# Masked values of head 6 on VectorE in a two-layer recurrent trunk

## The chip, the cores and the metric

The kernel runs on one core of a Trainium2 chip. The metric is the device time of one execution in microseconds, the median of several. The core has TensorE (PE, with its weight loads as PEld), VectorE (DVE), ScalarE (ACT), GpSimd (POOL) and SyncE (SP, which here only issues DMAs). Each engine takes its instructions in a fixed order of its own; semaphores join them.

## The reference

Two layers of a decoder trunk in float32, width 1024: a gated linear recurrence with convolution (layer 0), then HGRN2, a gated linear attention with a matrix state for each of 8 heads (layer 1), then a norm. There are 1024 prompt tokens from an empty state, and 8 sample sequences of 4 tokens each with a state of their own, so 1056 tokens in all. The part that the change touches is the state of the sample sequences in layer 1:

```python
def _hgrn_layer(x, g_norm, w_in, lb, o_gain, w_out, S0):
    ...
    q, f, iv, gate = jnp.split(u, 4, axis=-1)
    ...
    k = -jnp.expm1(log_g)
    v = iv.reshape(Bsz, T, H_B, DV_B)
    o, S_T = _hgrn2_chunked(q, k, v, log_g, S0)
    o = o * lax.rsqrt(jnp.mean(o * o, axis=-1, keepdims=True) + EPS) * o_gain.reshape(H_B, DV_B).astype(jnp.float32)
    y = (o.reshape(Bsz, T, INNER_B) * jax.nn.silu(gate)).astype(x.dtype)
    return x + y @ w_out, S_T.astype(x.dtype)
```

Within `_hgrn2_chunked` a state moves on by

```python
S_new = jnp.exp(last[:, :, 0, :])[..., None] * S + jnp.einsum(
    'bhsk,bhsv->bhkv', kc * jnp.exp(last - cum), vc)
```

For a sample sequence the sum over `s` runs over its four tokens alone.

## The kernel before

**Products.** Every large product is made of three: operands are split into a rounded part and a rest (`xh`, `xl`; `whi`, `wlo`), ACT makes the rounded part by a cast (L433, L1574, L1739) and DVE or POOL the rest by a subtraction (L374). In layer 1 the input projection of a head is done by `seven`, with seven products in place of eight (a Strassen-like scheme over halves of the tokens and of the weights). A cell of its order, such as `3a`, is product 3 for the first half of the columns: 12 matmuls of 264 columns (L289 to L291) into one bank. Three banks go round for these cells. DVE adds a cell's result to what stands in the SBUF (L1651) and so frees its bank. The order for the last section of a head is `GV`, where each `*` is a burst of small products for the head before:

```python
GV = "1a 1b 6a 2a 2b 6b * 7a 7b 5a 5b 4a * 3a 3b 4b"
```

**Head after head.** In the section of head `h` the four bursts carry work for head `h` (the decay of its attention, level by level, in `scale` L1176 and the masks of L1198 and L1201) and for head `h - 1`: `burst1` brings its sample keys and values into place (`samples`, L1314), `burst2` its prompt states (`states`, with the scan L1375 and L1377) and the first half of the new sample states (`advance(h - 1, 0)`), `burst3` its outputs and the second half (`advance(h - 1, 1)`), `burst4` the gated result. The bursts of head 7 are in its last `seven` section; what follows after that section is the output projection, whose operands are read back from DRAM (`yd`) into `xl`, `k` and other tiles and split there, with bursts between its products.

**Masked values.** The 32 sample tokens lie in 96 rows (three parts each). To get the states of four sequences with one product, `masked(i)` multiplies the values `vst` with a 0/1 mask `bm` for each sequence, two sequences an instruction: `vb <- vst * bm`, 96 x 256 numbers, two instructions for `i = 0` (from `values`, in `burst1`) and two for `i = 1` (from `advance(h, 0)`, in `burst2`, into the same `vb` after PE has read it). PE then multiplies `kst` by `vb` (L1386), and DVE adds that to the decayed state `si` (L1393). They are made by POOL for heads 0 to 6 and by DVE for head 7, the last.

**What sets the order.** `Flow` is a planner that runs when the program is built. Each operation is added with its engine, an estimate of its duration, what it reads and writes, and a priority. `run` plans the whole list forward, then back and forward again eight times, and then tries 3000 random moves with a fixed seed and keeps what its own model calls no later. The best order is written out, and the engines follow it as it stands. PE's main products keep the order in which they were added. So a change of one operation's engine or length can move many rows of the other engines, and it does not move PE's. The estimate for an operation on DVE with two SBUF inputs can be marked to count POOL's use of the same port (`both`); the masked values aren't marked.

Of the kernel before, what the change touches and what calls it, by code (L numbers as in the profile page):

```python
# [55 lines left out]
H = 8  # L56
# [201 lines left out]
def tile_trunk(ctx: ExitStack, tc: tile.TileContext, xT, xN, prm, hc, w0, wg, wo0, w1, wo1, s_in,  # L258
# [86 lines left out]
    with ExitStack() as l0:  # L345
# [12 lines left out]
        def dma(dst, src, r=(), w=(), prio=5, kb=180, q=Q, chain=None):  # L358
            fl.add("SP" if q is Q else "ACT", 0.45, lambda: q.dma_start(dst, src), r, w, prio, kb * (1.0 if r or fl.exact else 0.75),
                   line=chain)  # L360
# [4 lines left out]
        def dve(n, emit, r, w, prio=5, both=False, chain=None):  # L365
            own = 0.135 if "scalar_tensor_tensor" in emit.__code__.co_names else 0.085
            fl.add("DVE", own + 0.00107 * n if fl.exact else 0.13 + 0.0011 * n, emit, r, w, prio, both=both, line=chain)
# [695 lines left out]
    with ExitStack() as l1:  # L1063
# [40 lines left out]
        def pe(us, emit, r, w):  # L1104
            fl.add("PE", us, emit, r, w, 1, main=True)

        def two(*name):
            return [(*name, i) for i in range(2)]
# [205 lines left out]
        def samples(o, ok, s, sk, a, dss, key, low, whole=None):  # L1314

            ps = s[:, a:a + 128]

            pe(0.17, lambda: T.matmul(ps[:96], o, ident, start=True, stop=True), ((ok,),), (sk,))
            yield
            act(128, lambda: S.copy(dss, ps[:96]), (sk,), ((key,),), 2)  # L1320
            w = slice(32 * low, 32 * low + 32)
            dve(128, lambda: V.tensor_tensor(dss[w], ps[w], dss[w].bitcast(F32), op=ALU.subtract), (sk, (key,)), ((key,),), 2)
            if whole is not None:
                act(128, lambda: S.copy(whole, ps[:32]), (sk,), (("vts",),), 2)

        def values(h, s, sk):
            yield from samples(vrep, "vrep", s, sk, 192, vst, "vst", 2, vts)
            masked(0, h == H - 1)

        def masked(i, last=False):  # L1330

            n = [96, 2, 128]
            for j in range(2):
                o, q = vb[:, 2 * j:2 * j + 2], slice(4 * i + 2 * j, 4 * i + 2 * j + 2)
                e = V if last else G
                (dve if last else pool)(256, lambda o=o, q=q, e=e: e.tensor_tensor(o, vst.bitcast(F32)[:, None, :].to_broadcast(n), bm[:, q, None].to_broadcast(n),
                                                           op=ALU.mult), (("vst",),), (("vb",),), 3)
# [45 lines left out]
        def advance(h, i):  # L1383

            ps, pk = next(hg)
            pe(0.36, lambda: T.matmul(ps, kst, vb.rearrange("p b v -> p (b v)"), start=True, stop=True),  # L1386
               (("kst",), ("vb",)), (pk,))
            yield
            if i == 0:
                masked(1, h == H - 1)  # L1390
            for n in range(4):
                b = 4 * i + n
                dve(128, lambda n=n, b=b: V.scalar_tensor_tensor(  # L1393
                    si[:, b, :], si[:, b, :], gp[:, h % 2, 8 + b:9 + b], ps[:, n * 128:(n + 1) * 128], op0=ALU.mult, op1=ALU.add),
                    (pk, ("gp", h % 2, 1)), (("si", i),), 4)
            if i:
                dma(ss_out[h], si.rearrange("p b v -> p (b v)"), two("si"), (), 6, 512)
# [68 lines left out]
        def burst1(h):  # L1466
            s = next(hg)
            run(together([*([levels01(h, *s)] if h < H else []), *([keys_(h - 1, *s), values(h - 1, *s)] if h else [])]))

        def burst2(h):  # L1470
            s = next(hg)
            run(together([*([levels24(h, *s)] if h < H else []), *([states(h - 1, *s), advance(h - 1, 0)] if h else [])]))

        def burst3(h):
            s = next(hg)
            run(together([*([outs(h - 1, *s), advance(h - 1, 1)] if h else []), *([levels816(h, *s)] if h < H else [])]))
# [487 lines left out]
```

## Time and profile before

| | us |
|---|---|
| median of 3 runs | 1040.65 (1040.01 to 1040.68) |
| the profiled execution | 1039.88 |
| its span (first to last instruction) | 1038.1 |
| TensorE busy | 1028.7 |
| VectorE busy | 790.2 |
| ScalarE busy | 591.0 |
| GpSimd busy | 500.1 |
| idle time of TensorE that ended with a wait for another engine | 2.9, in 3 waits |

The trace is of the one profiled execution; its span leaves out 1.8 us of start and end that the device time has. Starts are in us from the span's start. A row of a timeline has start, duration, engine, line, operation, the tile written, an arrow and the tiles read, then shapes; "x2" stands for two instructions in a row, and in square brackets stands the idle time before it and what ended it. A row of the waits says which engine's instruction waited for which: the sum in us, how many times, and the longest. A row of the windows has, for each stretch, the busy time of PE, PEld, DVE, ACT and POOL, then the granted TensorE clock, the share of the DMA engines and GB/s.

### The profile page before, as it was taken

The numbers are of one execution on the slowest core, as the hardware profiler recorded it, in microseconds if no ns is written. First come the engines' busy times: TensorE is split into PE (matmuls) and PEld (weight loads), VectorE is DVE, ScalarE is ACT, GpSimd is POOL, SyncE is SP. The second block draws the span as 40 slices with busy tenths as digits, with TensorE's granted clock in tenths as the row PEclk, the third lists the DMA queues.
The fourth block names the chain that finished last, engine by engine and source line by source line (L and its number), as shares of the span: only waits on it lengthen the run. The fifth ranks groups of instructions, "written<-read, shape, count | busy, mean of one in ns | idle before, by whom it ended". The sixth has DMA issues, their size and how long they took to land.

```text
span 1038.1 us, 25405 instructions
## 1 busy us (share of the span) xinstructions
PE 1028.7 (99%) x9794; PEld 999.5 (96%) x9794; DVE 790.2 (76%) x1543; ACT 591.0 (57%) x1349; POOL 500.1 (48%) x579
## 2 busy tenths in 40 slices
PE   9999999999999999999999999999999999999997
PEld 9999999999999999999999999999999999999986
DVE  6898996887897699255498986878879696985436
ACT  6678657867675775234355474637464545752334
POOL 2344453354433365643627555555645455641544
PEclk9999999999999999999999999999999999999998
DMA  8611112124742595444554241413233332756204
GB/s 280 195 47 39 53 52 76 58 61 121 232 158 61 175 284 169 146 162 153 190 167 143 95 146 44 161 59 135 78 111 105 103 127 83 232 183 207 87 1 168
DMA packets 92809, 133.55 MB, mean 129 GB/s; under 512 B 11728, under 2 KB 70096, under 8 KB 92688
## 3 DMA queue, kind: packets, MB, share of 16 engines
q1 hardware_dynamic: 82896, 115.50, 35.4%
q10 hardware_dynamic: 9792, 16.43, 4.8%
q8 instruction: 77, 1.26, 0.5%
q14 instruction: 44, 0.36, 0.1%
HBM read 88.81 MB, written 38.20 MB: 122 GB/s over the span
## 4 chain that ended last, share of the span: by engine, by line
PE 98%; issue 1%; POOL 0%; DVE 0%; POOLq 0%; ACT 0%; DVEq 0%
PE mm L289 27%; PE mm L291 27%; PE mm L290 27%; PE hg L1194 2%; PE hg L291 1%; PE hg L651 1%; PE hg L289 1%; PE hg L290 1%; PE hg L1409 1%; PE hg L1411 1%; PE hg L1357 1%; PE mm L1357 1%; PE hg L813 1%; PE hg L1453 1%; PE hg L1279 0%
## 5 line engine op out<-in xcount | busy, mean ns | idle before, releaser
L289 PE MATMUL mm<-xh,whi 128*128 128x352 f32 (+1 forms) x1127 | 351.9, 312 | 0.0
L291 PE MATMUL mm<-xh,wlo 128*128 128x352 f32 (+1 forms) x1127 | 347.9, 309 | 0.0
L290 PE MATMUL mm<-xl,whi 128*128 128x352 f32 (+1 forms) x1127 | 347.3, 308 | 0.0
L374 POOL TENSOR_TENSOR wlo<-wraw,whi 128x256 fp32r<-128x256 f32 (+3 forms) x180 | 196.7, 1111 | 192.7 <-ACT whi L433 104.0
L290 PEld LDWEIGHTS mm<-xl,whi 128*128 128x128 f32 x1127 | 212.3, 188 | 1.7
L289 PEld LDWEIGHTS mm<-xh,whi 128*128 128x128 f32 x1127 | 212.0, 188 | 1.9
L291 PEld LDWEIGHTS mm<-xh,wlo 128*128 128x128 f32 x1127 | 211.8, 188 | 0.1
L289 PE MATMUL mm<-t,whi 128*128 128x264 f32 (+1 forms) x330 | 96.9, 294 | 1.3 <-DVE sg L1651 1.3
L583 DVE SCALAR_TENSOR_TENSOR k<-xb,prm_sb,k 128x352 f32<-128x352 f32 (+2 forms) x144 | 87.6, 616 | 13.0 <-ACT k L580 7.9
L290 PE MATMUL mm<-t,whi 128*128 128x264 f32 (+1 forms) x330 | 94.4, 286 | 0.0
L291 PE MATMUL mm<-t,wlo 128*128 128x264 f32 (+1 forms) x330 | 94.4, 286 | 0.0
L374 POOL TENSOR_TENSOR wlo<-R,whi 128x256 fp32r<-128x256 f32 x78 | 66.8, 882 | 43.9 <-ACT whi L1574 32.2
L666 POOL TENSOR_TENSOR k<-X 128x352 f32<-128x352 f32 x36 | 43.4, 1216 | 59.3 <-DVE R L667 42.0
L1651 DVE TENSOR_TENSOR k<-mm,k 128x264 f32<-128x264 f32 x118 | 49.7, 425 | 22.9 <-PE mm L291 22.4
L289 PEld LDWEIGHTS mm<-t,whi 128*128 128x128 f32 x330 | 62.1, 188 | 2.6 <-DVE sg L1651 1.8
L291 PEld LDWEIGHTS mm<-t,wlo 128*128 128x128 f32 x330 | 62.2, 188 | 0.0
L290 PEld LDWEIGHTS mm<-t,whi 128*128 128x128 f32 x330 | 62.2, 188 | 0.0
L433 ACT CAST whi<-wraw 128x512 fp32r<-128x512 f32 (+2 forms) x79 | 44.0, 571 | 25.0 <-PE mm L290 9.3
L289 PE MATMUL mm<-yh,whi 128*128 128x352 f32 x153 | 50.0, 327 | 0.0
L291 PE MATMUL mm<-yh,wlo 128*128 128x352 f32 x153 | 49.4, 323 | 0.0
L290 PE MATMUL mm<-yl,whi 128*128 128x352 f32 x153 | 49.4, 323 | 0.0
L647 ACT ACTIVATE R<-hg,smalls 128x352 f32<-128x352 f32 x72 | 37.5, 552 | 16.2 <-DVE R L687 9.3
(481 smaller groups left out, 2497.9 us busy)
## 6 DMA issues: line engine op xcount, KB each, us to landing
wraw<-in_w_dram SPq DMA_DIRECT2D x54, 256.0 KB, 3.2
wraw<-in_w_dram ACTq DMA_DIRECT2D x34, 256.0 KB, 3.5
wraw<-in_wo_dram SPq DMA_DIRECT2D x34, 192.0 KB, 2.5
R<-in_w_dram ACTq DMA_DIRECT2D x19, 256.0 KB, 2.7
si<-in_s_in_dram SPq DMA_DIRECT2D x8, 512.0 KB, 5.6
vt<-sg SPq DMA_DIRECT2D x8, 512.0 KB, 3.7
sg<-vt SPq DMA_DIRECT2D x32, 128.0 KB, 2.9
kt<-kt SPq DMA_DIRECT2D x8, 512.0 KB, 2.7
```

The lines of the kernel that those rows point to most:

```text
L289: T.matmul(out, wh, xh, start=first, stop=False, skip_group_check=more)
L290: T.matmul(out, wh, xl, start=False, stop=False, skip_group_check=more)
L291: T.matmul(out, wl, xh, start=False, stop=last, skip_group_check=more)
L374: emit = lambda: e.tensor_tensor(b, x, a.bitcast(F32), op=ALU.subtract)
L433: act(m, lambda: S.copy(hi[:, :m], raw[:, :m]), rk, (hk,), prio, chain=chains[0])
L583: dve(u, lambda src=src, dst=dst, sh=sh, k=k: V.scalar_tensor_tensor(dst, sh(src, k), pc("cw", 12 * k + m), dst, op0=ALU.mult, op1=ALU.add ...
L647: act(CH, lambda ps=ps, R=R, i=i, j=j, hb=hb, m=m: S.activation(R[:, i, j], ps[:, :CH], AF.Tanh, bias=hb[:, m:m + 1], scale=0.5), (pk, ("s ...
L651: fl.add("PE", 0.62, lambda ps=ps, i=i, c=c: T.matmul(ps[:96, :CH], gs[:, i, :], ST[:96, chunk(c)], start=True, stop=True), (("gs",), *((" ...
L666: pool(CH, lambda x=x, a=a, b=b: G.tensor_tensor(x, a.bitcast(F32), b.bitcast(F32), op=ALU.add), (ak, bk), (xk,), 3)
L1194: T.matmul(ps[32 * j:32 * j + 32, n * w:n * w + w], B[:, o:o + 32], q(slice(o, o + 32)), start=True, stop=True, tile_position=(0, 32 * j))
L1357: T.matmul(ps[:, n * 128:(n + 1) * 128], kt[:, 4 * i + n, :], vt[:, 4 * i + n], start=True, stop=True)
L1651: dve(QT, lambda: V.tensor_tensor(o[0], z[0], u[0], op=ALU.add), (z[1], u[1]), (o[1],), 0)
```

## The change

Head 6 is added to the heads whose masked values DVE makes, in both places where `masked` is called:

```diff
         def values(h, s, sk):
             yield from samples(vrep, "vrep", s, sk, 192, vst, "vst", 2, vts)
-            masked(0, h == H - 1)
+            masked(0, h >= H - 2)
...
             if i == 0:
-                masked(1, h == H - 1)
+                masked(1, h >= H - 2)
```

The function that is called stays as it is:

```python
def masked(i, last=False):

    n = [96, 2, 128]
    for j in range(2):
        o, q = vb[:, 2 * j:2 * j + 2], slice(4 * i + 2 * j, 4 * i + 2 * j + 2)
        e = V if last else G
        (dve if last else pool)(256, lambda o=o, q=q, e=e: e.tensor_tensor(o, vst.bitcast(F32)[:, None, :].to_broadcast(n), bm[:, q, None].to_broadcast(n),
                                                   op=ALU.mult), (("vst",),), (("vb",),), 3)
```

The planner orders the rest anew. PE's 6325 rows stay the same. First, DVE in the last section of head 7, around burst 2: `xl<-xl,xh` are subtractions for operands of the output projection, `attnd` and `attns` the masks of the attention, `a` the prompt's state scan, `sg<-mm,k` the additions for the cells 3a and 3b, and `k<-mm,k` an addition for an earlier cell. Before:

```order
L374 TENSOR_TENSOR xl<-xl,xh 128x352
L1198 COPY_PREDICATED attnd<-mask_91,hg 128x256
L374 TENSOR_TENSOR xl<-xl,xh 128x352
L1201 COPY_PREDICATED attns<-mask_90,hg 32x32
L1375 COPY a<-hg 128x128
L1377 SCALAR_TENSOR_TENSOR a<-a,gp,hg 128x128 x2
L374 TENSOR_TENSOR xl<-xl,xh 128x352
L1377 SCALAR_TENSOR_TENSOR a<-a,gp,hg 128x128
L1651 TENSOR_TENSOR sg<-mm,k 128x264
```

The same stretch of DVE now, from the first masked values of head 6 to the mask behind the addition for 3a:

```order
L1336 TENSOR_TENSOR vb<-vst,bm 96x256 x2
L1651 TENSOR_TENSOR k<-mm,k 128x264
L374 TENSOR_TENSOR t_5166<-t_5166 128x352
L1651 TENSOR_TENSOR k<-mm,k 128x264
L374 TENSOR_TENSOR t_5166<-R,t_5166 128x352
L374 TENSOR_TENSOR xl<-R,xh 128x352
L374 TENSOR_TENSOR xl<-xl,xh 128x352 x2
L1651 TENSOR_TENSOR k<-mm,k 128x264
L1198 COPY_PREDICATED attnd<-mask_90,hg 128x256
L374 TENSOR_TENSOR xl<-xl,xh 128x352
L1651 TENSOR_TENSOR sg<-mm,k 128x264
L1198 COPY_PREDICATED attnd<-mask_91,hg 128x256
```

The masked values (`vb`) are new there; the third `xl` and the addition for 3a come ahead of a mask, of `attns`, and of the whole state scan.

Second, POOL at the same place; `wlo` are the rests of weights, `ab` a small copy behind a product of burst 2. Before:

```order
L1336 TENSOR_TENSOR vb<-vst,bm 96x256 x2
L374 TENSOR_TENSOR t_5169<-wraw,t_5169 128x128
L374 TENSOR_TENSOR t_5168<-t_5168 128x352
L374 TENSOR_TENSOR wlo<-wraw,whi 128x128
L1235 COPY ab<-R 128x8x4
L374 TENSOR_TENSOR xl<-xl,xh 128x352
L1336 TENSOR_TENSOR vb<-vst,bm 96x256 x2
L374 TENSOR_TENSOR wlo<-wraw,whi 128x512 x2
```

POOL now:

```order
L374 TENSOR_TENSOR t_5169<-wraw,t_5169 128x128
L374 TENSOR_TENSOR t_5168<-t_5168 128x352
L374 TENSOR_TENSOR wlo<-wraw,whi 128x128
L1235 COPY ab<-R 128x8x4
L374 TENSOR_TENSOR xl<-xl,xh 128x352
L374 TENSOR_TENSOR wlo<-wraw,whi 128x512 x2
```

Both pairs are gone; the other rows keep their order.

Third, DVE some rows later, at the scaling of the decays for head 7 (L1176) and the first additions of the output projection (L1779); a piece of the difference:

```order
 L1176 TENSOR_TENSOR R<-R,sg 128x64x8
+L1336 TENSOR_TENSOR vb<-vst,bm 96x256 x2
+L374 TENSOR_TENSOR xl<-k,xh 128x352
 L1176 TENSOR_TENSOR a<-sg 128x64x8
+L374 TENSOR_TENSOR t_5166<-k,t_5166 128x352
+L1779 TENSOR_TENSOR ST<-mm,ST 128x352
+L1779 TENSOR_TENSOR R<-mm,R 128x352
```

The second pair of masked values now stands here, ahead of the last scaling, with one subtraction. ACT has some casts and copies in another order nearby; SP issues the same DMAs, some of them in another order.

## The prediction

> **What bounds the kernel now.** I read the busy times of the engines first, then the chain of work that ended last, then what TensorE (PE) waited for, then windows and the timelines of the stretch that they point to.
>
> ```profile
> PE 1028.7 (99%) x9794; PEld 999.5 (96%) x9794; DVE 790.2 (76%) x1543; ACT 591.0 (57%) x1349; POOL 500.1 (48%) x579
> PE 98%; issue 1%; POOL 0%; DVE 0%; POOLq 0%; ACT 0%; DVEq 0%
> PE mm L289 <- DVE sg L1651: 1.3, 1, 1.3
> PE hg L813 <- DVE nr L501: 1.0, 1, 1.0
> PE hg L1833 <- DVE sg L1823: 0.6, 1, 0.6
> ```
>
> PE is busy in 1028.7 of 1038.1 us and is 98% of the chain. Nothing done on VectorE (DVE) or GpSimd (POOL) can change the time except through an idle gap of PE. The waits of PE are three, 2.9 us in all: one each at L813 and L1833 (the norms of layer 0 and the end of the program, far from the change), and one at L289, where a product waited for DVE's L1651. This last lies in the section of head 6, whose masked values the change moves. The windows around it (busy PE, weight load, DVE, ACT, POOL) show that it is the only gap of PE there:
>
> ```profile
> 895.00:908.00 13.00, 13.00 (x295) 12.31 (x293) 12.23 (x24) 8.35 (x22) 10.90 (x12) 1.00 0.84 257
> 908.00:913.00 5.00, 3.73 (x31) 3.47 (x28) 4.52 (x9) 2.28 (x5) 4.44 (x6) 1.00 0.59 192
> 913.00:985.00 72.00, 72.00 (x648) 69.72 (x647) 43.45 (x103) 26.08 (x87) 25.39 (x28) 1.00 0.51 159
> ```
>
> Timeline of PE there: start, duration, line. The cell 3a ends with the matmul at 909.66, 3b with that at 911.13, and 4b begins at 912.68.
>
> ```profile
> 909.66 0.28 PE L291 MATMUL mm<-xh,wlo 128*128 128x264 f32 x1
> 909.78 0.28 PE L289 MATMUL mm<-xh,whi 128*128 128x264 f32 x1
> ...
> 911.13 0.28 PE L291 MATMUL mm<-xh,wlo 128*128 128x264 f32 x1
> 912.68 0.39 PE L289 MATMUL mm<-t,whi 128*128 128x264 f32 x1 [1.27 <-DVE sg L1651]
> 912.91 0.28 PE L290 MATMUL mm<-t,whi 128*128 128x264 f32 x1
> ```
>
> Matmuls normally start 0.12 us apart (909.66 to 909.78). From 911.13 to 912.91 two steps took 1.78 us instead of 0.24, so the stop cost **1.54 us**; the idle gap alone is 1.27. 4b writes into the bank from which DVE's L1651 adds up 3a's result. 3a had been finished since 909.66 + 0.28 = 909.94, so the delay is DVE's. Its queue, and POOL's beside it:
>
> ```profile
> 906.38 0.58 DVE L374 TENSOR_TENSOR xl<-xl,xh 128x352 fp32r<-128x352 f32 x1
> 906.88 0.43 DVE L1198 COPY_PREDICATED attnd<-mask,hg 128x256 f32<-128x256 uint8 x1
> 907.22 0.51 DVE L374 TENSOR_TENSOR xl<-xl,xh 128x352 fp32r<-128x352 f32 x1
> 908.41 0.18 DVE L1201 COPY_PREDICATED attns<-mask,hg 32x32 f32<-32x32 uint8 x1 [0.68 <-ACT os L1381]
> ...
> 909.47 2.56 DVE L374 TENSOR_TENSOR xl<-xl,xh 128x352 fp32r<-128x352 f32 x1
> 911.95 0.33 DVE L1377 SCALAR_TENSOR_TENSOR a<-a,gp,hg 128x128 f32<-128x128 f32 x1
> 912.21 0.42 DVE L1651 TENSOR_TENSOR sg<-mm,k 128x264 f32<-128x264 f32 x1
> ...
> 908.30 0.95 POOL L374 TENSOR_TENSOR xl<-xl,xh 128x352 fp32r<-128x352 f32 x1
> 909.22 1.18 POOL L1336 TENSOR_TENSOR vb<-vst,bm 96x256 fp32r<-96x256 f32 x2
> 910.36 1.29 POOL L374 TENSOR_TENSOR wlo<-wraw,whi 128x512 fp32r<-128x512 f32 x1
> 912.07 1.28 POOL L374 TENSOR_TENSOR wlo<-wraw,whi 128x512 fp32r<-128x512 f32 x1 [0.42 <-ACT whi L433]
> ```
>
> A subtraction that takes 0.51 at 907.22 took 2.56 at 909.47, 2.05 more. It read two tiles in the SBUF, as POOL's operations beside it do, and it ended at 912.03, 0.4 after POOL's unbroken row from 908.30 to 911.65 (the weight subtraction at 910.36 plus 1.29). Two of the operations in that row are the second pair of masked values (vb). L1651 stood behind it and started at 912.21; PE went on 0.47 later. The point from which the gap is gone follows: 4b's first matmul could start at 911.13 + 0.12 = 911.25, so L1651 must start by 911.25 − 0.47 = **910.78**.
>
> The Trainium skill states this lock too ("SBUF — State Buffer", section "Who interferes with whom"): a DVE instruction with two SBUF inputs contends with a GpSimd instruction that reads SBUF, and the one that has the port blocks the other for the whole instruction. The row at 909.47 goes further: the subtraction was held through more than one instruction.
>
> **The change part by part.** It moves four multiplications of head 6 from POOL to DVE, and the planner then orders much else anew. The durations on both engines are in the view of line 1336, and the places of the pairs in the timelines:
>
> ```profile
> L1336 POOL TENSOR_TENSOR vb<-vst,bm x28: 605/611/799, 572.6 to 909.8; 96x256 fp32r<-96x256 f32 x28
> L1336 DVE TENSOR_TENSOR vb<-vst,bm x4: 414/415/420, 948.5 to 960.9; 96x256 fp32r<-96x256 f32 x4
> 960.59 0.75 DVE L1336 TENSOR_TENSOR vb<-vst,bm 96x256 fp32r<-96x256 f32 x2
> 961.26 0.34 DVE L1393 SCALAR_TENSOR_TENSOR si<-si,gp,hg 128x128 f32<-128x128 f32 x1
> 903.11 0.45 DVE L1198 COPY_PREDICATED attnd<-mask,hg 128x256 f32<-128x256 uint8 x1
> 905.00 0.79 DVE L374 TENSOR_TENSOR xl<-R,xh 128x352 fp32r<-128x352 f32 x1
> 902.43 1.18 POOL L1336 TENSOR_TENSOR vb<-vst,bm 96x256 fp32r<-96x256 f32 x2
> 904.60 0.80 POOL L374 TENSOR_TENSOR t<-wraw,t 128x128 fp32r<-128x128 f32 x1 [0.98 <-ACT t L433]
> 905.56 1.02 POOL L374 TENSOR_TENSOR t<-t 128x352 fp32r<-128x352 f32 x1 [0.16 <-PE hg L1194]
> 906.54 0.73 POOL L374 TENSOR_TENSOR wlo<-wraw,whi 128x128 fp32r<-128x128 f32 x1
> ```
>
> POOL loses 4 x 0.611 = 2.44 us and DVE gains two pairs of 0.67 (960.59 to 961.26), 1.34 us. Neither counts by itself, since PE is the bound; what counts is when DVE reaches the addition for 3a.
>
> *POOL's row.* It loses the pair at 909.22. The weight subtraction of 910.36 can come up to 1.14 earlier (910.36 − 909.22); the cast on ACT that feeds it ran before, so nothing else holds it. The row then ends near 910.5.
>
> *DVE's queue ahead of 3a's addition.* The new order has the first pair before the third-last addition `k`, the third subtraction `xl` ahead, the addition for 3a right behind that, and `attnd` (mask_91), the copies for the state scan and `attns` behind the addition. From one such subtraction to the next instruction it is 0.43 (906.38 to 906.88 is 0.50, less the 0.07 that this row has over 0.51), so in before DVE could have gone on at 907.22 + 0.43 = 907.65. The pair adds 0.67, the third subtraction 0.43, and the mask that goes behind takes 0.34 away (906.88 to 907.22): 907.65 + 0.67 + 0.43 − 0.34 = **908.41**. The wait for ACT's `os` copy (0.68) goes too, since `attns` stands behind. 3a itself is ready only at 909.94. So DVE comes 1.5 us before the result and 910.78 − 908.41 = 2.37 us before the limit.
>
> *What a hold can take of that.* DVE's subtractions may again be held by POOL. The trace does not show the new overlap, so I bound it: nothing, or 2.05 as at 909.47. Even 2.05 leaves 0.32 of the 2.37. I take something between, near nothing, because the first pair comes right behind the mask copy of 903.11, where POOL, rid of its pair of 902.43, has nothing until ACT's cast lets it go on at 904.60, and the third subtraction meets POOL's row while it is still short. If that subtraction were held to the row's new end, 910.5, and ended 0.4 later as before, the addition would start near 911.0 and 0.2 of the 1.54 would be lost. This step is thus worth between −1.3 and −1.54; I take −1.54.
>
> *The additions that the first pair pushes back by 0.67.* They have cover: the latest, `k`, would end about 906.8 instead of 906.1, and PE works on its burst until 3a starts at 908.32 (the windows show PE without a gap there).
>
> *The second pair*, on DVE behind three of the scan scalings (L1176). These rows tell whether it is in time, with PE 1.54 earlier:
>
> ```profile
> 915.97 0.68 DVE L1176 TENSOR_TENSOR R<-R,sg 128x512 f32<-128x512 f32 x1
> 917.77 1.49 POOL L374 TENSOR_TENSOR xl<-k,xh 128x352 fp32r<-128x352 f32 x1 [4.43 <-ACT xh L1739]
> 923.16 0.50 PE L1386 MATMUL hg<-vb,kst 96*128 96x512 f32 x1
> ```
>
> From L1651 at 912.21 to L1176 at 915.97 DVE worked 3.76 without a break. In after that piece begins with 3a at about 910.0 and has 1.8 more in it (the mask 0.34, a copy and three scan steps at 0.33 or less each, `attns` 0.1): L1176 starts near 915.6. Three of them at about 0.6 and the pair (0.67) end near 918.1. PE needs the pair at 923.16 − 1.54 = 921.6: 3.5 us of cover, against a hold of 1.49 by the POOL row above. Without cover the cost would be as long as the lateness, one for one. The last scaling, `a<-sg`, comes behind that pair and one subtraction, so about 1.1 later, 919.2; its readers on PE come after L1386. DMA issues on SP are re-ordered (the loads of `yd` 3 and 2 change places, weights and `k` loads interleave differently), but no SP row is put ahead of the loads that 3a to 4b use; I cost it at nothing, within ±0.5.
>
> **Sum.** −1.54 and nothing new: the profiled execution goes from 1039.88 to 1038.3. The median of the three runs is 1040.65, 0.77 above the profiled one, so the median becomes 1040.65 − 1.54 = **1039.1 us**.
>
> **Rivals.** *The two engines merely swap who holds whom.* The stop stays, smaller: if the pair on DVE counted in full against what POOL saves, the addition would start at 912.21 − 1.14 + 0.67 − 0.26 (the scan step now behind it) = 911.48, 0.70 late, gain 0.84: 1039.8. For it speaks the row at 909.47; against it, that the pair on DVE is at about 903.5, in POOL's idle time. The Trainium skill has this as advice ("Perfetto Trace Analysis", section "Optimizing Scalar/DVE Operations"): GpSimd and DVE share an SBUF read port, "so offloading operations between those two might not help". *The stop keeps its size*, because another instruction of the new order is held ahead of 3a or 4b: 1040.65. *Slower: DVE becomes the bound at this place.* It is busy 12.23 of 13 us in 895–908 and gets more. From 908.41 it needs 912.21 − 908.41 = 3.80 us of holds to be later than before; it met about 2.4 in that stretch in before (2.05 at 909.47, 0.28 at the subtraction of 905.00, 0.07 at 906.38). If every POOL operation left there (0.80, 1.02, 0.73, 0.95, 1.29, 1.28, together 6.07) held it once in full, the addition would start at 914.5, PE would lose 3.7 instead of 1.54: 1042.8. That the change does not do what it says is excluded by the new order, which has all four on DVE.
>
> **Chances.** Stop gone 0.70 (1039.1, ±0.5 for the re-ordered rest); half gone 0.14 (1039.8); unchanged 0.07; slower 0.09 (1040.7 to 1042.8). The three runs span 0.67 us, so medians move by some tenths. The range goes from 1039.1 − 0.9 = 1038.2 to 1041.0; the upper end takes in the two middle cases, and the slower case beyond it and luck below share what is left out. A change of 0.2% (2.08 us, about what a measurement of this kernel can tell from none) would need 1038.57 or 1042.73. The forecast itself stays within it: faster 0.12 (the first case with 0.5 more from the rest or the spread), within 0.82, slower 0.06 (the upper part of the last case).
>
> **What would show it.** Right: no row L289 <- L1651 among PE's waits; PE busy 5.00 of 5.00 in the window 908–913; L1651 `sg<-mm,k` starting near 910.0; the DVE pair of 0.76 at about 903.5; the subtraction before 3a's addition nearer 0.5 than 2.5. Wrong: that subtraction or the pair held for over 2.37 us in sum; a new PE row at L1386, L1194 or L1357, which would mean that the second pair or the keys' round trip came late; or a gap at 4b's later neighbours.

## The result and the profile after

| | before | after |
|---|---|---|
| median | 1039.97 us (21 runs, 1039.13 to 1040.87) | 1038.50 us (21 runs, 1037.05 to 1039.14) |
| ratio | | 0.9985, 95% interval 0.9978 to 0.9991 |
| profiled execution, its span | 1039.88, 1038.1 | 1037.84, 1036.0 |

The kernel became 1.47 us faster, 0.15%. The whole interval of the ratio lies below 1, so the gain is clear of the spread; it is smaller than the 0.2% that the prediction's chances were drawn for. The forecast was −1.54 us, to 1039.1. Against the median of 1040.65 from the first three runs of before, the measured time is 2.15 lower; 0.7 of that is luck in the base, since those three were slower than most of the 21.

The waits of TensorE (PE) after, in us, times and longest; the row L289 <- L1651 is gone, and no new row has come in its place:

```profile
PE hg L813 <- DVE nr L501: 1.1, 1, 1.1
PE hg L1833 <- DVE sg L1823: 0.8, 1, 0.8
```

The window of the gap (busy PE, weight load, DVE, ACT, POOL) and PE's timeline at the passage from 3b to 4b. PE is busy in all of the 5 us, where before it was in 3.73, and 4b starts 0.12 behind the last matmul of 3b, the normal step of these matmuls:

```profile
908.00:913.00 5.00, 5.00 (x42) 4.95 (x41) 4.12 (x12) 2.79 (x7) 3.68 (x4) 1.00 0.63 209
911.10 0.28 PE L291 MATMUL mm<-xh,wlo 128*128 128x264 f32 x1
911.22 0.28 PE L289 MATMUL mm<-t,whi 128*128 128x264 f32 x1
911.34 0.29 PE L290 MATMUL mm<-t,whi 128*128 128x264 f32 x1
```

The queues of DVE and POOL that lead there, after:

```profile
903.28 1.02 DVE L1336 TENSOR_TENSOR vb<-vst,bm 96x256 fp32r<-96x256 f32 x2
...
905.78 1.25 DVE L374 TENSOR_TENSOR xl<-R,xh 128x352 fp32r<-128x352 f32 x1
906.96 1.21 DVE L374 TENSOR_TENSOR xl<-xl,xh 128x352 fp32r<-128x352 f32 x2
908.09 0.42 DVE L1651 TENSOR_TENSOR k<-mm,k 128x264 f32<-128x264 f32 x1
...
908.76 0.51 DVE L374 TENSOR_TENSOR xl<-xl,xh 128x352 fp32r<-128x352 f32 x1
909.95 0.43 DVE L1651 TENSOR_TENSOR sg<-mm,k 128x264 f32<-128x264 f32 x1 [0.68 <-PE mm L291]
...
911.42 0.43 DVE L1651 TENSOR_TENSOR sg<-mm,k 128x264 f32<-128x264 f32 x1
...
918.05 0.75 DVE L1336 TENSOR_TENSOR vb<-vst,bm 96x256 fp32r<-96x256 f32 x2
...
903.23 0.46 POOL L374 TENSOR_TENSOR t<-wraw,t 128x128 fp32r<-128x128 f32 x1 [0.92 <-ACT t L433]
905.56 1.10 POOL L374 TENSOR_TENSOR t<-t 128x352 fp32r<-128x352 f32 x1 [1.87 <-ACT t L1739]
906.62 0.73 POOL L374 TENSOR_TENSOR wlo<-wraw,whi 128x128 fp32r<-128x128 f32 x1
...
908.81 1.26 POOL L374 TENSOR_TENSOR xl<-xl,xh 128x352 fp32r<-128x352 f32 x1 [0.49 <-ACT xh L1739]
```

The reader is to see that DVE now waits for PE ahead of the addition for 3a (0.68 us idle, released by 3a's last matmul), where before PE waited for DVE. The subtraction that had taken 2.56 us takes 0.51: it starts at 908.76, 0.05 ahead of POOL's subtraction, and this time it is POOL's that gets longer (1.26 us; 0.95 in before).

One number compares all kernels at this place, since PE's work in between is the same: the time from PE's product for the first half of head 6's sample states (L1386 in burst 2) to that for the second half (burst 3). Before it is 923.16 − 907.97 = 15.19 us; after it is 921.58 − 907.94 = 13.64. The first row is of before (its second one, at 923.16, stands in the prediction), the other two are of after:

```profile
907.97 0.51 PE L1386 MATMUL hg<-vb,kst 96*128 96x512 f32 x1
...
907.94 0.51 PE L1386 MATMUL hg<-vb,kst 96*128 96x512 f32 x1
921.58 0.50 PE L1386 MATMUL hg<-vb,kst 96*128 96x512 f32 x1
```

So 1.55 us went here. The profiled spans differ by 2.1. The rest is almost all at PE's last two products (L1833), which took 1.22 us in before and 0.70 after. That is spread of single executions and not the change: in e10 below, a second profile of the changed kernel, they took 1.22.

### The profile page after: what moved, and what is told of

It is laid out like the page before. It is cut to its first block, busy times and chain, and to the rows that moved or that the text cites. A ratio compares the mean times of both kernels' runs of the same rounds, so it can differ in the third digit from the quotient of the medians.

```text
span 1036.0 us, 25403 instructions
## 1 busy us (share of the span) xinstructions
PE 1027.6 (99%) x9794; PEld 999.3 (96%) x9794; DVE 791.8 (76%) x1547; ACT 592.1 (57%) x1349; POOL 498.7 (48%) x575
## 3 DMA queue, kind: packets, MB, share of 16 engines
q8 instruction: 77, 1.26, 0.5%
## 4 chain that ended last, share of the span: by engine, by line
PE 98%; DVE 1%; issue 0%; POOL 0%; POOLq 0%; ACT 0%; ACTq 0%
PE mm L289 27%; PE mm L291 27%; PE mm L290 27%; PE hg L1194 2%; PE hg L651 1%; PE hg L289 1%; PE hg L291 1%; PE hg L290 1%; PE hg L1409 1%; PE hg L1411 1%; PE hg L1357 1%; PE hg L813 1%; PE mm L1357 1%; PE hg L1453 1%; PE hg L1365 0%
## 5 line engine op out<-in xcount | busy, mean ns | idle before, releaser
L289 PE MATMUL mm<-xh,whi 128*128 128x352 f32 (+1 forms) x1127 | 351.7, 312 | 0.0
L289 PEld LDWEIGHTS mm<-xh,whi 128*128 128x128 f32 x1127 | 211.9, 188 | 1.9
L289 PE MATMUL mm<-t,whi 128*128 128x264 f32 (+1 forms) x330 | 96.8, 293 | 0.0
L1651 DVE TENSOR_TENSOR k<-mm,k 128x264 f32<-128x264 f32 x118 | 49.6, 425 | 23.9 <-PE mm L291 22.8
L289 PEld LDWEIGHTS mm<-t,whi 128*128 128x128 f32 x330 | 62.1, 188 | 1.2 <-DVE sg L1651 0.5
L289 PE MATMUL mm<-yh,whi 128*128 128x352 f32 x153 | 50.0, 327 | 0.0
```

The source lines that it names most:

```text
L289: T.matmul(out, wh, xh, start=first, stop=False, skip_group_check=more)
L1651: dve(QT, lambda: V.tensor_tensor(o[0], z[0], u[0], op=ALU.add), (z[1], u[1]), (o[1],), 0)
```

## The experiments

The change does two things at once: four multiplications change the engine, and the planner, with these on another engine, writes out another order. **A**: the new order of DVE's queue closed the gap. **B**: POOL's relief did. **C**: the engines only swap who holds whom. Summary first; the column "stretch" is the time from L1386 to L1386. The median of before differed a little from one group of rounds to the next, so the ratios are to be compared and not the medians.

| kernel | stretch, us | median, us | ratio to before, 95% |
|---|---|---|---|
| before | 15.19 | 1039.97 (beside the change), 1039.61 (e1 to e4), 1039.68 (e5 to e8), 1039.80 (e9, e10) | |
| the change | 13.64 | 1038.50 | 0.9985 (0.9978 to 0.9991) |
| e1 its order, POOL multiplies | 13.62 | 1038.52 | 0.9988 (0.9979 to 0.9997) |
| e2 old order, DVE multiplies | 15.90 | 1040.53 | 1.0007 (0.9998 to 1.0016) |
| e3 before, addition for 3a ahead | 14.82 | 1039.57 | 0.9999 (0.9991 to 1.0008) |
| e4 before, POOL's pair later | 14.21 | 1038.70 | 0.9991 (0.9982 to 1.0000) |
| e5 before, both additions ahead | 13.64 | 1038.23 | 0.9984 (0.9976 to 0.9993) |
| e6 first pair only | 13.64 | 1038.44 | 0.9986 (0.9977 to 0.9996) |
| e7 second pair only | 13.64 | 1038.44 | 0.9985 (0.9976 to 0.9994) |
| e8 all heads | 13.6 | 1040.00 | 1.0001 (0.9992 to 1.0010) |
| e9 the change, additions ahead elsewhere | 13.6 | 1037.17 | 0.9977 (0.9968 to 0.9986) |
| e10 the change again, beside e9 | 13.64 | 1038.43 | 0.9987 (0.9979 to 0.9996) |

The intervals reach about 0.9 us to each side, so the medians alone don't tell e4 from e5. The finer comparisons rest on the stretch, which is read from one profiled execution each; in the two profiles of the changed kernel (the change and e10) it came out the same.

**e1: the order without the engine.** The planner still counts head 6's multiplications on DVE, but POOL carries them out.

```diff
-            masked(0, h >= H - 2)
+            masked(0, h >= H - 2, h == H - 1)
...
-        def masked(i, last=False):
+        def masked(i, last=False, own=False):
...
-                e = V if last else G
+                e = V if own else G
```

> The order that the planner makes for the changed kernel, with head 6's four multiplications carried out by POOL at the times planned for them. Theory A (the new order of DVE's queue, with the addition for 3a ahead of the scan, closes the gap): no PE wait at L289 on L1651, that addition at about 909.95 us, time 1.5 us below before. Theory B (what counts is that DVE and no longer POOL does them): POOL has the work again, the gap of about 1.3 us is back, time as before within 0.5 us.

Timeline of e1, POOL's first pair, then DVE's subtraction and addition:

```profile
903.39 1.18 POOL L1336 TENSOR_TENSOR vb<-vst,bm 96x256 fp32r<-96x256 f32 x2 [0.66 <-DVE vst L1322]
908.87 0.51 DVE L374 TENSOR_TENSOR xl<-xl,xh 128x352 fp32r<-128x352 f32 x1
910.36 0.43 DVE L1651 TENSOR_TENSOR sg<-mm,k 128x264 f32<-128x264 f32 x1 [0.97 <-PE mm L291]
```

The gap is gone with POOL doing all of the old work. B, put as "DVE and no longer POOL must do the work", has fallen, and the order that the planner made for the change is enough. Whether it is DVE's order or POOL's, e1 can't tell: POOL's second pair stands behind the weight subtractions here, so its place has changed, though not its engine. e5 separates the two.

**e2: the engine without the order.** The reverse: planned for POOL, carried out by DVE.

```diff
-            masked(0, h == H - 1)
+            masked(0, h == H - 1, h >= H - 2)
...
-                e = V if last else G
+                e = V if own else G
```

> The order of before, with head 6's four multiplications carried out by DVE at the places that they had in the program. POOL's row of 908.30 to 911.65 loses its pair, but the addition for 3a still stands behind the held subtraction, one multiplication and a scan step. Theory A: the subtraction ends near 910.9, the addition starts near 911.5 instead of 912.21, a PE gap of about 0.5 stays, time 0.8 us below before. Theory B: the gap goes, 1.5 us below. Theory C (the two engines only swap who holds whom): addition at 912 or later, no gain.

PE's wait, and DVE's queue, with POOL's weight subtraction beside it:

```profile
PE mm L289 <- DVE sg L1651: 1.8, 2, 1.1
...
909.52 1.64 DVE L374 TENSOR_TENSOR xl<-xl,xh 128x352 fp32r<-128x352 f32 x1
...
911.68 0.41 DVE L1651 TENSOR_TENSOR sg<-mm,k 128x264 f32<-128x264 f32 x1
...
912.28 1.39 DVE L1336 TENSOR_TENSOR vb<-vst,bm 96x256 fp32r<-96x256 f32 x1
...
914.37 0.42 DVE L1651 TENSOR_TENSOR sg<-mm,k 128x264 f32<-128x264 f32 x1
...
912.10 1.29 POOL L374 TENSOR_TENSOR wlo<-wraw,whi 128x512 fp32r<-128x512 f32 x1 [1.31 <-ACT whi L433]
```

At 3a it came out as A had it: addition at 911.68 (911.5 expected), gap 0.7 (0.5). What no theory had is the second gap, 1.05 us, at the next bank: one multiplication on DVE took 1.39 us (the one at 911.09 took 0.41), beside POOL's weight subtraction, and stood ahead of the addition for 3b. The stretch is 0.71 longer than before; the interval of the ratio (0.9998 to 1.0016) takes in 1, so the medians do not show a loss. So the engine alone, with the multiplications at these places in DVE's queue, brings nothing, and in the stretch it costs.

**e3: one row of before's order.** A function that reorders what the planner gives puts the addition for 3a ahead of the held subtraction. In the cut, `d` is the list of DVE's operations in order, `d[k]` is the held subtraction and `line` gives an operation's line.

```diff
-        for i in best[3]:
+        for i in placed(self, best[3]):
             self.ops[i][2]()
...
+    m = next(m for m in range(k, len(d)) if line(d[m]) == 1651)
+    order = [i for i in order if i != d[m]]
+    order.insert(order.index(d[k]), d[m])
```

> Before, with one DVE row moved: the addition for 3a stands ahead of the subtraction that was held for 2.05 us, nothing else changed, POOL still does the multiplications. Theory A: addition at 909.95, no PE wait there, 1.5 us below before, the same as the changed kernel. Theory B: POOL's load is what it was, the gap stays or turns up at the next addition (3b) or in the scan, gain below 0.5 us.

```profile
PE mm L289 <- DVE sg L1651: 0.9, 1, 0.9
...
910.17 0.43 DVE L1651 TENSOR_TENSOR sg<-mm,k 128x264 f32<-128x264 f32 x1 [0.43 <-PE mm L291]
910.52 1.70 DVE L374 TENSOR_TENSOR xl<-xl,xh 128x352 fp32r<-128x352 f32 x1
...
913.44 0.42 DVE L1651 TENSOR_TENSOR sg<-mm,k 128x264 f32<-128x264 f32 x1
```

A miss for A as it was put: the addition for 3a was in time, but the held subtraction and the state updates then delayed the addition for 3b (913.44), and the product behind 4b waited 0.94 us for that bank. The gap moved by one bank; only 0.37 us of the stretch was won, and the median did not move. That is what B had named for this run (the gap turns up at 3b, a gain below 0.5); e5 shows that it takes no relief of POOL to cure it.

**e4: POOL's pair later.** In before, POOL's second pair is put behind the two weight subtractions that followed it. `p` is the list of POOL's operations, `v` the places of that pair in it.

```diff
...
+    order = [i for i in order if i not in (p[v[0]], p[v[1]])]
+    k = order.index(p[v[1] + 2]) + 1
+    return order[:k] + [p[v[0]], p[v[1]]] + order[k:]
```

> Before, with two POOL rows moved: the second pair of multiplications stands behind the next two weight subtractions instead of ahead of them; DVE's order is untouched. If the pair lengthened the hold (theory A and B), the subtraction on DVE ends about 1.1 us sooner, at 910.9, the addition for 3a starts near 911.2, the PE gap shrinks to about 0.2 and the time falls by 1.1 us. If the subtraction is held by whatever POOL does (theory C), it still ends near 912.0 and the time stays.

```profile
PE mm L289 <- DVE sg L1651: 0.3, 1, 0.3
910.25 1.56 DVE L374 TENSOR_TENSOR xl<-xl,xh 128x352 fp32r<-128x352 f32 x1
```

The subtraction on DVE, unmoved, took 1.56 instead of 2.56 us: one of the 2.05 us of the hold was POOL's pair. The stretch fell by 0.98 (1.1 expected), the gap to 0.27; the interval of the ratio ends at 1.0000. So a second lever exists on POOL's side, and it too is a matter of place: no multiplication changed its engine.

**e5: both additions.** As e3, with the addition for 3b put right behind the held subtraction. POOL's and ACT's queues are those of before.

```diff
...
+    m = next(i for i in range(m + 1, len(d)) if line(d[i]) == 1651)
+    order = [i for i in order if i != d[m]]
+    order.insert(order.index(d[k + 1]), d[m])
```

> Before, with two DVE rows moved: the addition for 3a ahead of the held subtraction (as in the run where that alone was moved) and the addition for 3b right behind it, ahead of the scan step and the four state updates. POOL still does all multiplications of head 6. Theory A (the order of the two additions against the held subtraction is the whole cause): subtraction ends near 912.2, addition for 3b starts there, 0.3 us ahead of the point where the next product needs its bank; no PE wait at L289, time 1.3 to 1.5 us below before. Theory B (work has to leave POOL): the gap turns up once more further on, gain below 0.5 us.

The two additions with the subtraction between them, then PE's two products that bound the stretch:

```profile
911.03 0.43 DVE L1651 TENSOR_TENSOR sg<-mm,k 128x264 f32<-128x264 f32 x1 [0.43 <-PE mm L291]
911.38 1.70 DVE L374 TENSOR_TENSOR xl<-xl,xh 128x352 fp32r<-128x352 f32 x1
913.00 0.42 DVE L1651 TENSOR_TENSOR sg<-mm,k 128x264 f32<-128x264 f32 x1
...
909.02 0.51 PE L1386 MATMUL hg<-vb,kst 96*128 96x512 f32 x1
922.66 0.50 PE L1386 MATMUL hg<-vb,kst 96*128 96x512 f32 x1
```

The hold is still there (1.70), but it stands between the two additions and nothing waits for it: 13.64, as with the change. Two rows of DVE's order are worth all of it, with POOL doing all of its old work in its old order.

**e6 and e7: one pair each**, planned anew. The cut is e6's; `masked(1, ...)` is as in before there.

```diff
-            masked(0, h == H - 1)
+            masked(0, h >= H - 2)
```

> Only the first pair (from burst 1) of head 6 goes to DVE, planned anew; the second stays on POOL in its row between the split of xl and the weight subtractions. The new order has the addition for 3a ahead of the scan and behind the third subtraction. Theory A: that order decides, addition at 910 to 911, gap 0 to 0.3, time 1.2 to 1.5 us below before. Theory B (the second pair in POOL's row holds DVE): the subtraction is held by about 2 us again, addition near 911.5 or later, gain below 0.8 us.

> Only the second pair (from burst 2) goes to DVE, planned anew; POOL's row loses its pair. The new order has a scaling, two subtractions and one scan step ahead of the addition for 3a, and four more rows between it and the addition for 3b. Theory A: addition for 3a near 910.5, for 3b near 912.4, at its limit: gap 0 to 0.4, gain 1.0 to 1.5 us. Theory B (the pair off POOL is what counts): gain 1.5 us whatever stands ahead of the additions.

e7 has the same edit at `masked(1, ...)` alone. The additions for 3a and 3b, in e6, then in e7:

```profile
910.23 0.43 DVE L1651 TENSOR_TENSOR sg<-mm,k 128x264 f32<-128x264 f32 x1 [0.34 <-PE mm L291]
912.02 0.41 DVE L1651 TENSOR_TENSOR sg<-mm,k 128x264 f32<-128x264 f32 x1
...
910.40 0.43 DVE L1651 TENSOR_TENSOR sg<-mm,k 128x264 f32<-128x264 f32 x1 [0.38 <-PE mm L291]
911.99 0.43 DVE L1651 TENSOR_TENSOR sg<-mm,k 128x264 f32<-128x264 f32 x1
```

In both DVE waits for PE ahead of the first, and both have the whole gain, though e6 leaves POOL the pair that lengthened the hold. Either edit leads the planner to an order in which the third subtraction comes sooner and most of the scan stands behind the addition for 3a. e7 does not part A from B, since both expected about 1.5 us; e6 does, since B expected a hold of about 2 us again and the subtraction took 0.82.

**e8: all heads.** `masked(1, ...)` is changed in the same way.

```diff
-            masked(0, h == H - 1)
+            masked(0, True)
```

> DVE makes the masked values of all eight heads, planned anew; 28 multiplications leave POOL, DVE gains about 9.4 us in the whole. Theory A: TensorE waited for none of the earlier ones, so nothing more than in the changed kernel comes of it: 1.5 us below before (both additions stand ahead of the scan again), if the new order has no new gap. Theory B (each pair off POOL is worth something): more than 3 us below before. Theory C (DVE is the fuller engine, 76% against 48%): new PE waits on DVE in the heads before, time above before.

The stretch is short here too, but the time is that of before. The loss is spread over the heads before, in gaps mostly too short for the list of waits. (The list has one long row that before has not, 1.2 us at L326, near 22 us in layer 0. The order of e8 first differs from that of before near 503 us, and rows of 0.2 to 0.6 at this line are in e2, e4 and e9 too, whose edits lie in layer 1, so it is taken as spread of a single execution.) At cell 4b in the section of head 2, e8 first, then before:

```profile
635.68 0.28 PE L291 MATMUL mm<-xh,wlo 128*128 128x264 f32 x1
636.18 0.39 PE L289 MATMUL mm<-t,whi 128*128 128x264 f32 x1 [0.22 <-DVE sg L1651]
636.41 0.28 PE L290 MATMUL mm<-t,whi 128*128 128x264 f32 x1
...
635.01 0.28 PE L291 MATMUL mm<-xh,wlo 128*128 128x264 f32 x1
635.19 0.39 PE L289 MATMUL mm<-t,whi 128*128 128x264 f32 x1
635.41 0.29 PE L290 MATMUL mm<-t,whi 128*128 128x264 f32 x1
```

From the last matmul of 3b to the second of 4b it should be 0.24 us. Before has 0.40, so 0.16 lost; e8 has 0.73, 0.49 lost. Read in the same way, before lost 0.16 to 0.22 in four such places, 0.76 in all, and e8 0.18 to 0.49 in six, 2.21 in all. The difference, 1.45, eats what was won at head 6. So the third case of the expectation, DVE as the fuller engine, named the right place for the new losses (why the additions came later there is not shown); the longer time that it expected is not shown, since the ratio is 1.0001.

**e9: the same cure for the other heads**, on top of the change: in the sections of heads 2 to 6 the addition for 3a goes ahead of one scaling. e10 is the change again, in the same rounds.

```diff
...
+    for k in range(2, len(d)):
+        if line(d[k]) == 1651 and line(d[k - 1]) == 1176 and line(d[k - 2]) == 1377:
+            order.remove(d[k])
+            order.insert(order.index(d[k - 1]), d[k])
```

> The changed kernel, with the addition for 3a put ahead of the scaling (0.68 us) that stands before it in the sections of heads 2 to 6, where TensorE lost 0.16 to 0.22 us at cell 4b each (below what the list of waits names) in before. Theory A (order of DVE's queue): these losses go, 4 x 0.2 = 0.8 us below the changed kernel, 2.3 us below before. If they came from something else than that queue, the time is that of the changed kernel.

> The changed kernel once more, on the chip and in the rounds of the run before it, for comparison: 1.5 us below before.

```profile
633.97 0.42 DVE L1651 TENSOR_TENSOR sg<-mm,k 128x264 f32<-128x264 f32 x1
634.31 0.68 DVE L1176 TENSOR_TENSOR R<-R,sg 128x512 f32<-128x512 f32 x1
...
634.82 0.28 PE L291 MATMUL mm<-xh,wlo 128*128 128x264 f32 x1
634.94 0.28 PE L289 MATMUL mm<-t,whi 128*128 128x264 f32 x1
635.06 0.29 PE L290 MATMUL mm<-t,whi 128*128 128x264 f32 x1
```

The small losses are gone (0.24 from the last matmul of 3b to the second of 4b), and this version beats both: 1037.17 us, 1.26 below the change in the same rounds (0.8 expected). In the two profiles the cells 4b of these heads give 0.58 of the gain and the whole way from the first L1386 to that of head 6 gives 1.16; the rest is in further short steps of PE there. Why those got shorter stays open.

## Why the prediction was right, and where it was not

- *The gap is DVE's late addition for 3a, worth 1.54 us.* Right: 1.55 in the stretch, 1.47 in the medians.
- *The hold of 2.05 us came from POOL's row with the pair in it.* Right in kind: with the pair moved away the same subtraction took 1.56 (e4), so about half of the hold was the pair's; the rest was there with the weight subtraction alone beside it. (The prediction puts the gap in the section of head 6; it is head 7's, where head 6's masked values are used.)
- *DVE reaches the addition at 908.41 plus holds of near nothing.* The size was off. By the prediction's own count, 0.43 from the start of a subtraction to the next instruction, DVE could go on at 908.76 + 0.43 = 909.19, 0.78 later. The reason given, that the first pair falls where POOL has nothing to do until 904.60, failed: with ACT's order changed POOL's weight subtraction came at 903.23, and the pair took 1.02 instead of 0.75; more was lost at the `xl` subtraction of 905.78 (1.25; 0.79 at 905.00 in before). The bound of 2.05 with its limit of 2.37 covered it, and 3a is ready only at 909.95, so nothing of it reached PE.
- *POOL's row ends near 910.5.* It ended at 911.32 (a weight subtraction at 910.03, 1.29 long), since POOL's `xl` subtraction waited for ACT's cast until 908.81 and took 1.26. So if DVE's subtraction had been held to the end of that row, more than the 0.2 us that the prediction gives would have been lost.
- *The additions that the pair pushes back: the latest, `k`, ends about 906.8.* It ended at 908.51. The sum counted the pair alone and left out the two `xl` subtractions that the new order puts ahead of this addition, and the holds. PE had no gap all the same, so the cover was enough.
- *The third subtraction near 0.5.* Right, but with luck in the size: it started 0.05 ahead of POOL's subtraction, and that one got longer. In e6, where it started behind POOL's, it took 0.82, and 3a's addition still had to wait 0.34 for PE.
- *The second pair ends near 918.1, with PE needing it at 921.6.* It ended at 918.80 and PE took it at 921.58; no wait. Cover was enough.
- *POOL's shorter row* as a term of the sum: not needed. The prediction joined POOL's relief and the new order in one sum; e5 shows that DVE's order alone brings all of it, e1 that the change's order does so with POOL at work, and e2 that the engine alone brings none. e4 shows that a shorter row of POOL is a lever of its own, worth 0.98.
- *The rivals.* The rival "half gone" was 0.84 of gain; e2, the run nearest to its condition, lost 0.71 in the stretch instead. The rival "slower, DVE becomes the bound" named a mechanism that e2 shows for the old order (a held instruction on DVE ahead of an addition). e8 shows late additions for the other heads, but not from holds at the place shown: its addition at 635.70 stood behind a scaling of 0.68 us, as long as in before. The Trainium skill's advice that offloading between the two engines might not help ("Perfetto Trace Analysis", section "Optimizing Scalar/DVE Operations") agrees with e2 (ratio 1.0007) and e8 (1.0001), where no gain came of it.

## What to carry to other kernels

When an order is planned, an edit that changes one operation's engine is also a draw of a new order; before crediting the engine, run the new order with the old engine and the old order with the new one. Where one engine bounds a kernel, look for the instruction that frees what it needs next (here the addition that frees a bank) and put it ahead of everything in its queue that can be held by another engine; moving one such instruction may only move the gap to the next buffer. A list of waits hides what is short: read start-to-start times at the places that recur.

## What the runs showed of the hardware

A DVE subtraction that POOL delayed mostly went on after the POOL instruction that was running, even with more POOL work right behind it: at 905.78 in after, where POOL's subtraction ran from 905.56 to 906.66 and its next began at once, it took 1.25 us. It was so too in e1 at 904.03, where it began during a masked multiplication: it took 0.93 us and ended 0.38 after that multiplication.

In a few places it was held through more than one. In before at 909.47 it was held through the rest of the pair and the weight subtraction (2.56 us), and in e3 and e5 from the last 0.1 us of the pair through the weight subtraction (1.70 us each). Masked multiplications are not needed for it: in e1 a subtraction at 905.23 began in the last 0.05 us of one POOL subtraction and was held through the next two (1.75 us; 0.51 for the same one in before):

```profile
905.23 1.75 DVE L374 TENSOR_TENSOR t<-R,t 128x352 fp32r<-128x352 f32 x1
...
905.24 0.93 POOL L374 TENSOR_TENSOR t<-t 128x352 fp32r<-128x352 f32 x1
906.13 0.45 POOL L374 TENSOR_TENSOR wlo<-wraw,whi 128x128 fp32r<-128x128 f32 x1
```

The Trainium skill ("SBUF — State Buffer", section "Who interferes with whom") tells of a block for the whole of one instruction; these four cases go beyond it. What decides between one instruction and several stays open.
